# The scores across two chunks in two 32-column pieces: a hybrid recurrence and ConvFFN layer on one core

## The chip, the cores and the metric

The kernel runs on one core of a Trainium2 chip. The metric is the device time of one execution in microseconds (us). Given are the times of three executions of the kernel before and one profiled execution, from which all rows below come.

## The reference

One layer over 2048 tokens of width 1024, all in fp32. After a modulated RMSNorm one projection feeds two gated linear attentions, 4 HGRN heads with 128 key features and 4 GLA heads with 64, each with 128 value features. Both are computed in chunks of 64 tokens:

```python
b = jnp.cumsum(g, axis=3)
scores = jnp.einsum('bhncd,bhnsd->bhncs', q * jnp.exp(b - ref), k * jnp.exp(ref - b))
scores = jnp.where(causal, scores, 0.0)
o = jnp.einsum('bhncs,bhnse->bhnce', scores, v)
...
s0 = jnp.zeros((B, H, DK, DV), jnp.float32)
_, s_prev = lax.scan(step, s0, (decay, u))
o = o + jnp.einsum('bhncd,nbhde->bhnce', q * jnp.exp(b), s_prev)
```

The heads are normed, gated and projected, and a second norm, an up projection with a causal convolution of width 3, a gated product and a down projection follow.

## The kernel before

The 2048 tokens are four sub-sequences of T = 512, each of NT = 4 token tiles of P = 128 tokens, that is two chunks of CH = 64. Two sub-sequences go through the token mixer (`plan_A`), then both through the ConvFFN (`plan_ffn`), and this twice. The large projections (L363, L849, L884, L1220, L1551) are matmuls in float32r with 512 moving columns, in three passes over operands split into a high and a low part; the split of the weights is a cast on ScalarE (L128) and a subtraction on VectorE (L131).

In `plan_A` a list of steps holds the projections, and the stages of the heads are hung between them by step number (`at`, `at_half`). A `Unit` is one HGRN head, or two GLA heads that share 128 partitions (features 0 to 63 and 64 to 127). So a sub-sequence has 8 heads in 6 units. `stage_b` makes `kx` on POOL (L592), the keys of the first chunk of every tile with their decay to the chunk's end; `stage_c` makes `qx` on VectorE, the queries of the second chunk with their decay from its start. `stage_d` calls `scores` for the unit's first head and `stage_d2` for the second head of a GLA unit.

`scores` (L642) works over two chunks at once: for each token tile `p` it makes a 128 x 128 block of scores, keys on the PSUM partitions, queries on the columns, all four tiles of a head in one PSUM bank. The scores within a chunk (L649) are made in four pieces of HC = 32 key columns: each has a named place in the array, `tile_position=(lo, r0)`, writes the 32 partitions from `r0` on, and has 64 moving columns for `r0` = 0 and 64 and 32 moving columns for `r0` = 32 and 96 (the upper triangle alone is made). The scores across the two chunks, the first chunk's keys against the second chunk's queries (L657), are one piece of 64 key columns and 64 moving columns without a named place. All of these matmuls are in plain fp32. POOL then clears an SBUF tile (L665) and VectorE copies the valid scores into it under a mask (L670).

`stage_d2` makes the chunk pairs' state updates (L680) and VectorE forms the three states between the tiles (L690); `stage_e` makes the outputs from scores and values (L706) and from queries and states (L707).

The order on ScalarE and SyncE is that of the program. The order of TensorE, VectorE and POOL in the main loop is made by the framework when the program is built, from the program's order and its own estimates of durations. The framework also places the semaphores.

Of the kernel before, what the change touches and what calls it, by code (L numbers as in the profile page):

```python
# [17 lines left out]
P = 128  # L18
# [8 lines left out]
CH = 64  # L27
HC = CH // 2
# [34 lines left out]
def kernel(  # L63
# [26 lines left out]
    act, vec, pool, pe, sp = nc.scalar, nc.vector, nc.gpsimd, nc.tensor, nc.sync  # L90
# [14 lines left out]
    def slot(dt=F32):  # L105
        return slots.tile([P, T], dt, tag="s", name="s")
# [4 lines left out]
    def bank():  # L111
        return psp.tile([P, T], F32, tag="ps", name="ps")
# [433 lines left out]
    class Unit:  # L546
# [95 lines left out]
        def scores(self, hd):  # L642
            kt_t, qt_t = self.e2, self.e1
            lo, hi, v, col = hd["lo"], hd["hi"], hd["v"], hd["col"]
            sb = bank()
            for p in range(NT):
                for r0 in range(0, P, HC):
                    c0, c1 = p * P + r0, p * P + (r0 // CH + 1) * CH
                    pe.matmul(  # L649
                        sb[r0 : r0 + HC, c0:c1],  # L650
                        lhsT=kt_t[lo:hi, c0 : c0 + HC],
                        rhs=qt_t[lo:hi, c0:c1],
                        start=True,
                        stop=True,
                        tile_position=(lo, r0),
                    )
                pe.matmul(  # L657
                    sb[0:CH, p * P + CH : (p + 1) * P],
                    lhsT=self.kx[lo:hi, p, :],
                    rhs=self.qx[lo:hi, p, :],  # L660
                    start=True,
                    stop=True,
                )
            sct = slot().rearrange("p (n t) -> p n t", t=P)
            pool.memset(sct, 0.0)  # L665
            sv = sb.rearrange("p (n t) -> p n t", t=P)
            for c0 in range(0, P, HC):
                rs = slice(c0, c0 + HC)
                mk = mask[rs, c0:P].unsqueeze(1).broadcast_to([HC, NT, P - c0])
                vec.copy_predicated(sct[rs, :, c0:P], mk, sv[rs, :, c0:P])  # L670
            self.sct.append(sct)
# [1311 lines left out]
```

## Time and profile before

| | |
|---|---|
| three executions, us | 2404.80, 2405.66, 2408.79 (median 2405.66) |
| profiled execution, us | 2408.29 |
| its span, first to last instruction, us | 2406.6 |
| mean granted TensorE clock | 0.987 of full speed |
| busy TensorE matmul / VectorE / ScalarE / POOL, us | 2330.0 / 1841.0 / 1179.5 / 344.0 |

Engines: PE is TensorE's matmuls, PEld its weight loads, DVE VectorE, ACT ScalarE, POOL GpSimd, SP SyncE. L657 is line 657 of the kernel. An fp32 matmul shows as two loads and two matmul records. The matmuls are pipelined, so that records overlap and their ends are modelled; the starts are what the reader should compare. Waits are inferred from the semaphores' events.

### The profile page before, as it was taken

To read this page: it belongs to the slowest core of one execution; us is meant where nothing else is said; L and a number is where in the kernel's file an instruction comes from. 1 tells how busy PE (TensorE), PEld (TensorE's weight loads), DVE (VectorE), ACT (ScalarE), POOL (GpSimd) and SP (SyncE) were. 2 spreads that over 40 slices of the span, in tenths; PEclk is the share of its full clock that TensorE was granted. 3 is DMA by queue.
4 is the path that set the end of the run, shared out by engine and by line. 5 is a ranking of instruction groups with operands and counts; after the bars stand their busy time and mean duration, and the time that the engine had idled before them with its cause. 6 is when DMAs were issued, how large, how long until landed. Compare 5 with 4: busy or idle time off the path is not lost.

```text
span 2406.6 us, 32511 instructions
## 1 busy us (share of the span) xinstructions
PE 2330.0 (97%) x12054; PEld 1920.2 (80%) x12054; DVE 1841.0 (76%) x2787; ACT 1179.5 (49%) x2095; POOL 344.0 (14%) x312
## 2 busy tenths in 40 slices
PE   8999999999999999999989999999999999999996
PEld 6878787887888888888777878888878888888885
DVE  6786778868788788887876676566697787897778
ACT  5643544366454545544445354543654545545453
POOL 3342234110000000000124213320100000000001
PEclk9999999999999999999999999999999999999998
DMA  8332352323222247996434034221232222589761
GB/s 303 110 119 106 111 228 96 128 72 133 93 92 92 101 139 245 347 336 216 169 140 152 17 114 167 71 80 54 96 127 79 101 96 101 180 283 378 249 205 70
DMA packets 148703, 360.80 MB, mean 150 GB/s; under 512 B 17544, under 2 KB 20024, under 8 KB 148544
## 3 DMA queue, kind: packets, MB, share of 16 engines
q1 hardware_dynamic: 148544, 358.73, 41.9%
q8 instruction: 94, 1.54, 0.3%
q14 instruction: 65, 0.53, 0.1%
HBM read 293.65 MB, written 65.01 MB: 149 GB/s over the span
## 4 chain that ended last, share of the span: by engine, by line
PE 76%; DVE 14%; ACT 3%; issue 3%; DMA 3%; POOL 0%; SPq 0%; DVEq 0%; ACTq 0%; POOLq 0%
PE ps L1220 26%; PE ps L1551 14%; PE ps L363 13%; PE ps L849 12%; PE ps L884 3%; DVE wlo L131 2%; DVE s L131 2%; PE ps L657 1%; PE ps L649 1%; DMA s<-in_w_ada 1%; PE ps L706 1%; PE ps L707 1%; ACT whi L128 1%; DVE s L1666 1%; PE ps L680 1%
## 5 line engine op out<-in xcount | busy, mean ns | idle before, releaser
L1220 PE MATMUL ps<-s,whi 128*128 128x512 f32 x1904 | 585.9, 389 | 2.4 <-DVE big L1320 2.4
L363 PE MATMUL ps<-s,whi 128*128 128x512 f32 x1568 | 493.2, 396 | 11.8 <-ACT whi L128 11.8
L131 DVE TENSOR_TENSOR wlo<-big,whi 128x1024 fp32r<-128x1024 f32 (+3 forms) x290 | 343.1, 1193 | 137.7 <-ACT whi L128 134.2
L1220 PEld LDWEIGHTS ps<-s,whi 128*128 128x128 f32 x1904 | 357.2, 188 | 77.4 <-DVE big L1320 3.2
L1551 PE MATMUL ps<-s,whi 128*128 128x512 f32 (+1 forms) x1272 | 384.9, 384 | 4.7 <-DVE s L131 3.0
L1220 PE MATMUL ps<-s,wlo 128*128 128x512 f32 x952 | 370.0, 389 | 2.4 <-DVE wlo L1213 2.4
L363 PEld LDWEIGHTS ps<-s,whi 128*128 128x128 f32 x1568 | 295.4, 190 | 77.5 <-ACT whi L128 14.4
L128 ACT CAST whi<-big 128x1024 fp32r<-128x1024 f32 (+3 forms) x298 | 275.2, 939 | 148.0 <-PE ps L1551 27.9
L849 PE MATMUL ps<-whi,s 128*128 128x512 f32 (+2 forms) x1280 | 340.8, 355 | 6.2 <-ACT whi L128 6.2
L455 POOL TENSOR_TENSOR s<-s 128x512 f32<-128x512 f32 (+1 forms) x69 | 102.8, 1490 | 1552.6 <-ACT s L454 1134.2
L363 PE MATMUL ps<-s,wlo 128*128 128x512 f32 x784 | 308.1, 394 | 2.8 <-DVE wlo L131 2.8
L1551 PEld LDWEIGHTS ps<-s,whi 128*128 128x128 f32 x1272 | 237.3, 189 | 54.6 <-DVE s L131 4.7
L849 PEld LDWEIGHTS ps<-whi,s 128*128 128x128 f32 x1280 | 218.9, 190 | 38.5 <-ACT whi L128 7.9
L1551 PE MATMUL ps<-s,wlo 128*128 128x512 f32 (+1 forms) x636 | 244.1, 384 | 5.0 <-DVE wlo L131 4.9
L849 PE MATMUL ps<-wlo,s 128*128 128x512 f32 (+2 forms) x640 | 205.6, 352 | 7.0 <-DVE wlo L131 7.0
L1220 PEld LDWEIGHTS ps<-s,wlo 128*128 128x128 f32 x952 | 178.7, 188 | 40.6 <-DVE wlo L1213 3.2
L363 PEld LDWEIGHTS ps<-s,wlo 128*128 128x128 f32 x784 | 148.9, 190 | 35.7 <-DVE wlo L131 4.1
L1213 DVE TENSOR_TENSOR wlo<-big,whi 128x1024 fp32r<-128x1024 f32 (+1 forms) x136 | 145.4, 1085 | 5.9 <-ACT whi L1209 5.7
L1209 ACT CAST whi<-big 128x1024 fp32r<-128x1024 f32 (+1 forms) x136 | 127.5, 939 | 37.4 <-DVE big L1197 33.7
L1551 PEld LDWEIGHTS ps<-s,wlo 128*128 128x128 f32 x636 | 119.8, 188 | 30.2 <-DVE wlo L131 7.3
L1265 DVE SCALAR_TENSOR_TENSOR big<-big,cw_sb 128x1024 f32<-128x1024 f32 x68 | 87.4, 1285 | 68.4 <-ACT big L1257 68.4
L849 PEld LDWEIGHTS ps<-wlo,s 128*128 128x128 f32 x640 | 114.0, 190 | 22.5 <-DVE wlo L131 8.9
(220 smaller groups left out, 3294.4 us busy)
## 6 DMA issues: line engine op xcount, KB each, us to landing
big<-in_wt SPq DMA_DIRECT2D x230, 512.0 KB
s<-td SPq DMA_DIRECT2D x110, 256.0 KB
big<-in_wd SPq DMA_DIRECT2D x72, 384.0 KB
s<-actd SPq DMA_DIRECT2D x98, 256.0 KB
s<-in_w_ada SPq DMA_DIRECT2D x96, 256.0 KB
big<-in_wd SPq DMA_DIRECT2D x72, 320.0 KB
actd<-big SPq DMA_DIRECT2D x34, 512.0 KB
td<-s SPq DMA_DIRECT2D x54, 256.0 KB
```

Source lines behind the costliest of these rows:

```text
L128: act.copy(hi, src)
L131: (lo_engine or vec).tensor_tensor(lo, src, hi.bitcast(F32), op=ALU.subtract)
L363: pe.matmul(pt, lhsT=wv[:, k * P : (k + 1) * P], rhs=hv, start=(n == 0), stop=(n == 3 * KD - 1))
L455: engine.tensor_tensor(acc, acc, sq, op=ALU.add)
L649: pe.matmul(sb[r0 : r0 + HC, c0:c1], lhsT=kt_t[lo:hi, c0 : c0 + HC], rhs=qt_t[lo:hi, c0:c1], start=True, stop=True, tile_position=(lo, r0),)
L849: pe.matmul(pt[:, 0 : c1 - c0], lhsT=hv[:, tt * P : (tt + 1) * P], rhs=wv[:, k2 * stride + c0 : k2 * stride + c1], start=(m == 0), stop=(m ...
L884: pe.matmul(pout[j][0], lhsT=wv[:, k * P : (k + 1) * P], rhs=hv, start=(k == 0 and m == 0), stop=(k == KD - 1 and m == 2),)
L1209: act.copy(dst[f][0][:, 0:n], src[f][:, 0:n])
L1213: vec.tensor_tensor(lo[:, 0:n], src[f][:, 0:n], hi[:, 0:n].bitcast(F32), op=ALU.subtract)
L1220: pe.matmul(pt, lhsT=wv[:, c0 : c0 + P], rhs=hv, start=(start and n == 0), stop=(n == 11), skip_group_check=not start)
L1265: vec.scalar_tensor_tensor(t_, src[:, 1 : 1 + D], w1, t_, op0=ALU.mult, op1=ALU.add)
L1551: pe.matmul(pt[:, cols], lhsT=wv[:, ki * P : (ki + 1) * P], rhs=hv[:, cols], start=(start and n == 0), stop=(n == 3 * np_ - 1), skip_group ...
```

## The change

The piece across the chunks becomes two pieces of 32 key columns, each with a named place in the array, in the same way as the pieces within a chunk. The second loop runs over `r0` = 0 and 32; both pieces stream the same `qx`.

```diff
@@ -654,13 +654,15 @@
                         stop=True,
                         tile_position=(lo, r0),
                     )
-                pe.matmul(
-                    sb[0:CH, p * P + CH : (p + 1) * P],
-                    lhsT=self.kx[lo:hi, p, :],
-                    rhs=self.qx[lo:hi, p, :],
-                    start=True,
-                    stop=True,
-                )
+                for r0 in range(0, CH, HC):
+                    pe.matmul(
+                        sb[r0 : r0 + HC, p * P + CH : (p + 1) * P],
+                        lhsT=self.kx[lo:hi, p, r0 : r0 + HC],
+                        rhs=self.qx[lo:hi, p, :],
+                        start=True,
+                        stop=True,
+                        tile_position=(lo, r0),
+                    )
             sct = slot().rearrange("p (n t) -> p n t", t=P)
             pool.memset(sct, 0.0)
             sv = sb.rearrange("p (n t) -> p n t", t=P)
```

## Rows read from the trace of the kernel before

**Rows 1.** The page: the chain that ended last, by engine and by line.
```profile
PE 76%; DVE 14%; ACT 3%; issue 3%; DMA 3%; POOL 0%; SPq 0%; DVEq 0%; ACTq 0%; POOLq 0%
PE ps L1220 26%; PE ps L1551 14%; PE ps L363 13%; PE ps L849 12%; PE ps L884 3%; DVE wlo L131 2%; DVE s L131 2%; PE ps L657 1%; PE ps L649 1%; DMA s<-in_w_ada 1%; PE ps L706 1%; PE ps L707 1%; ACT whi L128 1%; DVE s L1666 1%; PE ps L680 1%
```

**Rows 2.** Windows of two mixer stages: length; busy PE, PEld, DVE, ACT, POOL; clock; DMA.
```profile
136.00:250.00 114.00, 112.07 (x865) 91.47 (x863) 82.44 (x179) 50.18 (x136) 28.58 (x33) 1.00 0.30 107
400.00:515.00 115.00, 114.04 (x887) 94.11 (x886) 87.30 (x201) 47.01 (x129) 17.41 (x21) 1.00 0.34 115
```

**Rows 3.** Two source lines: records, shortest/median/longest ns, first and last start, forms.
```profile
L649 PE MATMUL ps<-s x1024: 192/216/243, 141.2 to 1657.1; 128*32 128x64 f32 x65, 64*32 64x64 f32 x63, 64*32 64x32 f32 x22, 128*32 128x32 f32 x21
...
L657 PE MATMUL ps<-s x256: 218/244/270, 141.5 to 1657.4; 128*64 128x64 f32 x64, 64*64 64x64 f32 x64
```

**Rows 4.** TensorE's timeline, first HGRN block (start us, us, rows*columns, moving operand, count).
```profile
141.22 0.31 PE L649 MATMUL ps<-s 128*32 128x64 f32 x8
141.47 0.33 PE L657 MATMUL ps<-s 128*64 128x64 f32 x2
141.73 0.31 PE L649 MATMUL ps<-s 128*32 128x64 f32 x8
...
143.23 0.50 PE L849 MATMUL ps<-whi,s 128*128 128x512 f32 x1
```

**Rows 5.** The same in windows of 0.02 us: last passes of a group alone.
```profile
141.31 0.23 PE L649 MATMUL ps<-s 128*32 128x64 f32 x2
...
141.32 0.22 PE L649 MATMUL ps<-s 128*32 128x64 f32 x1
...
141.57 0.22 PE L657 MATMUL ps<-s 128*64 128x64 f32 x1
```

**Rows 6.** TensorE's timeline, first GLA block.
```profile
165.64 0.31 PE L649 MATMUL ps<-s 64*32 64x64 f32 x8
165.88 0.32 PE L657 MATMUL ps<-s 64*64 64x64 f32 x2
...
167.62 0.50 PE L363 MATMUL ps<-s,whi 128*128 128x512 f32 x1
```

**Rows 7.** TensorE's timeline: first of 16 output passes, and what follows them.
```profile
155.15 0.27 PE L706 MATMUL ps<-s 128*128 128x128 f32 x1
...
156.85 0.48 PE L849 MATMUL ps<-whi,s 128*128 128x512 f32 x1
```

**Rows 8.** TensorE's timeline: state updates of a GLA unit, 16 passes in two column positions.
```profile
172.54 1.09 PE L680 MATMUL ps<-s 128*64 128x128 f32 x16
...
173.36 0.28 PE L680 MATMUL ps<-s 128*64 128x128 f32 x2
173.57 0.50 PE L363 MATMUL ps<-s,whi 128*128 128x512 f32 x1
```

**Rows 9.** Windows around the GLA units, sub-sequences 1 to 3; columns as in rows 2.
```profile
164.90:178.30 13.40, 13.40 (x143) 10.39 (x142) 13.14 (x20) 4.41 (x7) 3.40 (x6) 1.00 0.56 210
...
420.00:442.20 22.20, 22.20 (x206) 17.92 (x204) 21.55 (x38) 10.05 (x25) 7.81 (x9) 1.00 0.35 120
...
1352.30:1365.30 13.00, 13.00 (x140) 10.02 (x139) 12.56 (x19) 4.33 (x6) 3.25 (x5) 1.00 0.01 2
```

**Rows 10.** Timelines: a GLA unit's last state (L690) and the load taking it (L707).
```profile
177.27 0.34 DVE L690 SCALAR_TENSOR_TENSOR sprev<-sprev,dp,ps 128x128 f32<-128x128 f32 x1
...
178.35 0.30 PEld L707 LDWEIGHTS ps<-sprev,s 128*128 128x128 f32 x2
...
438.92 0.34 DVE L690 SCALAR_TENSOR_TENSOR sprev<-sprev,dp,ps 128x128 f32<-128x128 f32 x1
...
439.35 0.30 PEld L707 LDWEIGHTS ps<-sprev,s 128*128 128x128 f32 x2
...
1363.00 0.73 DVE L690 SCALAR_TENSOR_TENSOR sprev<-sprev,dp,ps 128x128 f32<-128x128 f32 x2
...
1365.60 0.30 PEld L707 LDWEIGHTS ps<-sprev,s 128*128 128x128 f32 x2
```

## The prediction

> **What bounds the kernel now.** The page comes first. The chain that ended last is TensorE for 76% of the span, and the score matmuls stand in it by name: L657, the piece across the chunks, and L649, the pieces within a chunk, hold about 1% each [rows 1]. Then the busy time by stage: in the stretch of the token mixer that holds eight score blocks TensorE is busy 112.07 of 114 us, VectorE 82.44, and the second sub-sequence looks the same [rows 2]. So here TensorE's queue sets the pace, and VectorE has a quarter of the time free on average. Then the two lines: L649 has 1024 matmul records, L657 256 [rows 3]. The loops issue 512 and 128, so each fp32 matmul here runs as two passes. 32 units (4 sub-sequences, 8 heads) each run one block of four token tiles: 8 + 2 passes per tile, 40 per block.
>
> **Where a block's time goes.** In the timeline a block of an HGRN head takes 2.01 us, from 141.22 to 143.23, in four equal periods of 0.50 us: eight passes of L649, two of L657, eight of L649 again [rows 4]. In narrower windows the last of the eight L649 passes starts at 141.32, only 0.10 us after the first, and then nothing starts until L657 at 141.47. The second pass of L657 starts at 141.57, and the next tile's L649 only at 141.73 [rows 4, 5]. So a period is 0.10 us in which the diagonal passes start, 0.15 us to the change of form, 0.10 us between the passes of L657, and 0.16 us to the change back. The GLA heads do the same with 64 rows: 165.64 to 167.62, 1.98 us [rows 6]. After the first piece no semaphore can explain the gaps: they repeat to 0.01 us in every tile, and only the form of the piece changes there (32 or 64 columns of the array).
>
> **What a pass costs.** Sixteen fp32 passes with 128 moving columns start between 155.15 and 156.85: 0.106 us each, 0.83 ns a column [rows 7]. So 64 moving columns are 0.053 us and 32 are 0.027. The wide second pass of a tile starts some 0.08 us after the first (141.31 against 141.22, rounded) [rows 4, 5]: one load of 32 columns, 0.027, and one pass of 0.053. The last pass of a form started 0.15 us before the next form; less its own 0.053 this leaves 0.10 us of emptying. That is paid twice a tile.
>
> **The change, part by part.**
> Removed: 128 matmuls, so 256 loads of 64 columns and 256 passes. Added: 256 matmuls, so 512 loads of 32 columns and 512 passes of 64 moving columns. The passes are those of L649 in form and position. The operands (kx, qx), the bank, the wait of the first piece and the reader (L670) stay; no DMA and no step on another queue is added or moved.
> The eight changes of form in a block become one at its start and one at its end, which are there already. What then bounds a tile is the busiest column position. Position 0 gets two diagonal passes and two cross passes of 64 columns, 4 x 0.053 = 0.213 us; position 32 gets 2 x 0.027 + 2 x 0.053 = 0.160; positions 64 and 96 get 0.107 and 0.053. If positions run side by side, a block is 0.027 + 16 x 0.053 + 0.10 = 0.98 us.
> The nearest row for such a stream is L680 of the GLA units: 16 passes of 128 moving columns in two named column positions, all of one form. Its last starts at 173.36, and the block takes 172.54 to 173.57, 1.03 us [rows 8]. My rule gives 0.053 + 8 x 0.106 + 0.10 = 1.00, so it is 0.03 short, and one after the other they would need 1.7 us. I therefore take 1.00 us for the new block.
> Gain on TensorE's queue: 16 x (2.01 - 1.00) + 16 x (1.98 - 1.00) = 31.8 us.
> Bounds: no block can be shorter than position 0's passes, 0.85 us, which gives at most 36.6 us. If the cross pieces start only when the diagonal ones are done, but without emptying, a tile is 0.10 + 0.053 + 0.08 + 0.06 = 0.29 us, a block 1.26, the gain 23.5 us. I take the value at the L680 row because it has the same structure.
>
> A rule that speaks for the whole gap: the Trainium skill, "TensorEngine Tiling (Array Packing)", Key Properties, says that a change of the tiling mode drains TensorE while a change of tile within a mode doesn't. The rows show the gaps and not their cause; by that rule all of them go.
>
> **What is late next.** The 31.8 us are gained only where TensorE's later work isn't waiting for VectorE. There is one place per sub-sequence where VectorE is full: 13.14 of 13.40 us from 164.9, 21.55 of 22.20 from 420, 12.56 of 13.00 from 1352.3 [rows 9], with two GLA blocks (2 us of gain) inside. Behind them TensorE's load for L707 takes the state that VectorE's L690 writes. In the first sub-sequence that state is done at 177.27 + 0.34 = 177.61 and taken at 178.35: 0.74 us of room, so 1.2 of the 2 us are lost. In the second it is 439.26 against 439.35, room 0.09, so 1.9 are lost. In the third 1363.73 against 1365.60, room 1.87, so some 0.2 are lost, and 0.3 is taken for each of the third and the fourth [rows 10]. Sum of losses 3.7 us. Elsewhere VectorE's gaps are waits for TensorE, so it follows. The weight splits and the DMAs are issued behind the same steps and move along.
> Result: 31.8 - 3.7 = 28.1 us. The profiled execution took 2408.29 us (span 2406.6), so 2380.2 for it. The median of the runs is 2.6 us lower, and I state 2378 us against that median.
>
> **The rivals.**
> *The gap isn't the form's.* If the emptying belongs to going from the diagonal pieces to the cross pieces (same bank, the same 64 partitions), it stays: a tile is 0.10 + 0.15 + 0.09 + 0.15 = 0.49 us, and 128 tiles save 1 to 2 us: 2404, no measurable change. Against it: L680's passes go through one bank and the same partitions with no gap [rows 8]. Chance 5%.
> *Slower: the gap stays, and the two cross pieces also run one after the other,* because both stream the same moving operand qx. Place: TensorE's queue between a tile's last diagonal pass and the next tile. A tile is then 0.10 + 0.15 + 0.027 + 4 x 0.053 + 0.10 = 0.59 us against 0.50, and 128 tiles add 11.5 us: 2417. It decides only if both hold, since without the gap four serial passes (0.24 us) still cost less than today's 0.40 from 141.32 to 141.73. Against it: in L649 passes of four positions start within 0.10 us, where one after the other they would need 0.32 [rows 4, 5]. Chance 4%.
> *Loads block each other.* If a load waited for every running pass, each of 24 load-and-pass pairs in a tile would stand alone, 12 x 0.027 + 8 x 0.053 + 4 x 0.027 = 0.86 us, +46 us: 2452. Rows 4 and 5 show eight loads and passes begun in 0.10 us, so it doesn't hold for column positions. Chance 1%.
> The Trainium skill, "TensorE: Matmul & The Clock Gate", Part 3, states that rule: loads overlap running matmuls only where the row group differs, and all pieces of a block here share theirs. The L649 rows disagree.
> *Half of it:* no overlap between cross and diagonal, the lower bound above; 23.5 less 3.7 gives 2386. Chance 8%.
> That the change does nothing can be left out: the forms 128 x 64 and 64 x 64 at L657 are in the trace, and the added pieces ask for another.
>
> **How the numbers follow.** The forecast, a block near 1.0 us with losses of 2 to 8 us, has the other 82%: 2372 to 2384. The upper bound of the gain, 36.6 less 2, gives 2371; the half case with twice the losses gives 2390. The build also orders VectorE's, TensorE's and POOL's queues anew, and one displaced step costs what the waits around here cost, 1 to 2 us. So the range is 2370 to 2390. About 0.2% (4.8 us) is what a measurement of this kernel can tell from no change. Faster by more than that: forecast and half case, 0.90. Within: the first rival, 0.05. Slower: the two others, 0.05.
>
> **What would show it.** Right: L657 has 512 matmul records with 32 columns at about 0.22 to 0.24 us each; a block goes from 2.0 to about 1.0 us; the next line's first pass comes 0.15 us after the block's last; L707 gains short waits for L690 in the first and second sub-sequence; VectorE's busy sum doesn't change. Wrong: periods of some 0.5 us remain in the block, or the blocks shrink and TensorE waits for VectorE as much longer behind them.

## The result and the profile after

The changed kernel takes 2380.48 us (median of four executions, 2378.33 to 2382.34) against 2407.22 us before (four, 2404.80 to 2409.31): a ratio of 0.9895, with a 95% interval of 0.9883 to 0.9907, 26.7 us less. The forecast was 2378, in a range of 2370 to 2390, against the 2405.66 us that were known of the kernel before. The profiled execution took 2378.33 us, with a span of 2376.6 against 2406.6 before, 30.0 less.

The page of the changed kernel, which answers to rows 1: the score lines are no longer among the fifteen that lead the chain (lines behind 657 have moved by two: L851 is the L849 of before, L709 the L707, L692 the L690; L658 holds the cross pieces).

```profile
PE 74%; DVE 16%; ACT 4%; issue 4%; DMA 2%; POOL 0%; SPq 0%; DVEq 0%; ACTq 0%; POOLq 0%
PE ps L1222 26%; PE ps L1553 14%; PE ps L363 13%; PE ps L851 11%; PE ps L886 3%; DVE wlo L131 3%; DVE s L131 2%; DMA s<-in_w_ada 1%; PE ps L709 1%; PE ps L708 1%; ACT whi L128 1%; DVE s L1668 1%; PE ps L682 1%; PE ps L816 1%; DVE s L1579 1%
```

The source view of the cross pieces, which answers to rows 3: 512 passes in place of 256, all with 32 columns of the array.

```profile
L658 PE MATMUL ps<-s x512: 216/219/244, 139.6 to 1626.3; 128*32 128x64 f32 x86, 64*32 64x64 f32 x85
```

TensorE's timeline of the changed kernel, an HGRN block and the first GLA block, which answer to rows 4 and 6. The lines L649 and L658 now alternate every few hundredths of a microsecond:

```profile
209.60 0.30 PE L649 MATMUL ps<-s 128*32 128x64 f32 x7
209.70 0.22 PE L658 MATMUL ps<-s 128*32 128x64 f32 x1
...
210.35 0.22 PE L649 MATMUL ps<-s 128*32 128x64 f32 x1
210.38 0.30 PE L658 MATMUL ps<-s 128*32 128x64 f32 x3
210.62 0.50 PE L851 MATMUL ps<-whi,s 128*128 128x512 f32 x1
...
163.31 0.30 PE L649 MATMUL ps<-s 64*32 64x64 f32 x7
...
164.31 0.50 PE L363 MATMUL ps<-s,whi 128*128 128x512 f32 x1
```

The HGRN block takes 1.01 us from its first pass to the next line by the unrounded starts (210.62 - 209.60 = 1.02 by the rounded rows), where it took 2.00, and the GLA block 1.01 (1.00 by the rows), where it took 1.98. No gap is left inside.

**Where the 30 us come from.** TensorE issues the same other matmuls in both kernels, in the same order. So the start of each can be compared in the two traces, and the gain read as it grows. It grows in steps of 0.99 us behind each HGRN block and 0.97 behind each GLA block. The exception is the first block: there the build's new order put one projection pass (L851) between 40 of the 48 passes and the last 8, so it pays two more changes of form and gains 0.63:

```profile
140.17 0.33 PE L649 MATMUL ps<-s 128*32 128x32 f32 x3
140.42 0.50 PE L851 MATMUL ps<-whi,s 128*128 128x512 f32 x1
140.85 0.24 PE L649 MATMUL ps<-s 128*32 128x64 f32 x2
...
141.10 0.50 PE L851 MATMUL ps<-whi,s 128*128 128x512 f32 x1
```

The sum is 15 x 0.99 + 16 x 0.97 + 0.63 = 31.0 us. Between the blocks of a sub-sequence the gain falls again, by 1.10 us in the first, 1.95 in the second, 0.28 in the third and 0.28 in the fourth: 3.6 us. That leaves 27.4. (The 0.98 and 1.65 us named in an expectation below count only the passes that wait; behind each such stop the next pass comes 0.10 us later too, and that isn't made up.) The other 2.6 us of this pair of profiles lie outside these stretches, as the sum of rises and falls of up to 2 us. Most of them stand where the granted clock differs, as windows of both traces show (length, TensorE's busy time and matmuls, granted clock, DMA share and GB/s). Of the kernel before:

```profile
126.00:140.00 14.00, 11.06 (x39) 0.76 0.02 4
238.00:252.00 14.00, 12.07 (x56) 1.00 0.12 39
1425.00:1443.00 18.00, 16.07 (x69) 0.91 0.09 29
```

And of the changed kernel, at the same places of the program:

```profile
126.00:139.00 13.00, 10.63 (x43) 0.87 0.06 18
230.00:245.00 15.00, 13.05 (x55) 0.90 0.11 36
1404.00:1422.00 18.00, 16.05 (x77) 1.00 0.09 30
```

A mean of 0.76 is a mixture of the two levels, 2.4 and 1.2 GHz. TensorE is idle for 1.9 us or more in each of these windows in both kernels, but the lower level isn't at the same ones. Part of what the clock gives or takes comes back at a later wait: at some 1780 us of the kernel before, the changed one gained 1.1 us because it stood at the lower level for a shorter time there, and it lost 1.2 right behind, where its L1222 waited for a cast on ScalarE (L1211).

### The profile page after: what moved, and what is told of

Read it like the earlier page. It is cut to its first block, busy times and chain, and to the rows that moved or that the text cites. A ratio compares the mean times of both kernels' runs of the same rounds, so it can differ in the third digit from the quotient of the medians.

```text
span 2376.6 us, 33021 instructions
## 1 busy us (share of the span) xinstructions
PE 2299.3 (97%) x12310; PEld 1904.7 (80%) x12310; DVE 1838.8 (77%) x2787; ACT 1179.6 (50%) x2095; POOL 341.0 (14%) x312
## 4 chain that ended last, share of the span: by engine, by line
PE 74%; DVE 16%; ACT 4%; issue 4%; DMA 2%; POOL 0%; SPq 0%; DVEq 0%; ACTq 0%; POOLq 0%
PE ps L1222 26%; PE ps L1553 14%; PE ps L363 13%; PE ps L851 11%; PE ps L886 3%; DVE wlo L131 3%; DVE s L131 2%; DMA s<-in_w_ada 1%; PE ps L709 1%; PE ps L708 1%; ACT whi L128 1%; DVE s L1668 1%; PE ps L682 1%; PE ps L816 1%; DVE s L1579 1%
## 5 line engine op out<-in xcount | busy, mean ns | idle before, releaser
L1222 PE MATMUL ps<-s,whi 128*128 128x512 f32 x1904 | 586.2, 389 | 3.7 <-DVE big L1322 2.4
L363 PE MATMUL ps<-s,whi 128*128 128x512 f32 x1568 | 492.4, 396 | 11.8 <-ACT whi L128 11.8
L131 DVE TENSOR_TENSOR wlo<-big,whi 128x1024 fp32r<-128x1024 f32 (+3 forms) x290 | 343.6, 1194 | 134.4 <-ACT whi L128 130.6
L1222 PEld LDWEIGHTS ps<-s,whi 128*128 128x128 f32 x1904 | 357.0, 188 | 79.2 <-DVE big L1322 3.2
L1222 PE MATMUL ps<-s,wlo 128*128 128x512 f32 x952 | 369.9, 389 | 2.4 <-DVE wlo L1215 2.4
L363 PEld LDWEIGHTS ps<-s,whi 128*128 128x128 f32 x1568 | 294.9, 190 | 77.6 <-ACT whi L128 14.4
L851 PE MATMUL ps<-whi,s 128*128 128x512 f32 (+2 forms) x1280 | 339.9, 354 | 5.5 <-ACT whi L128 5.5
L363 PE MATMUL ps<-s,wlo 128*128 128x512 f32 x784 | 307.8, 394 | 3.1 <-DVE wlo L131 3.1
L851 PEld LDWEIGHTS ps<-whi,s 128*128 128x128 f32 x1280 | 218.2, 189 | 37.8 <-ACT whi L128 7.2
L851 PE MATMUL ps<-wlo,s 128*128 128x512 f32 (+2 forms) x640 | 205.0, 351 | 6.5 <-DVE wlo L131 6.5
L1222 PEld LDWEIGHTS ps<-s,wlo 128*128 128x128 f32 x952 | 178.7, 188 | 40.4 <-DVE wlo L1215 3.2
L363 PEld LDWEIGHTS ps<-s,wlo 128*128 128x128 f32 x784 | 148.6, 189 | 36.3 <-DVE wlo L131 4.9
L1211 ACT CAST whi<-big 128x1024 fp32r<-128x1024 f32 (+1 forms) x136 | 127.5, 939 | 37.4 <-DVE big L1199 33.8
L851 PEld LDWEIGHTS ps<-wlo,s 128*128 128x128 f32 x640 | 113.6, 189 | 21.9 <-DVE wlo L131 8.5
```

Source lines behind the costliest of these rows:

```text
L131: (lo_engine or vec).tensor_tensor(lo, src, hi.bitcast(F32), op=ALU.subtract)
L363: pe.matmul(pt, lhsT=wv[:, k * P : (k + 1) * P], rhs=hv, start=(n == 0), stop=(n == 3 * KD - 1))
L851: pe.matmul(pt[:, 0 : c1 - c0], lhsT=hv[:, tt * P : (tt + 1) * P], rhs=wv[:, k2 * stride + c0 : k2 * stride + c1], start=(m == 0), stop=(m ...
L1211: act.copy(dst[f][0][:, 0:n], src[f][:, 0:n])
L1222: pe.matmul(pt, lhsT=wv[:, c0 : c0 + P], rhs=hv, start=(start and n == 0), stop=(n == 11), skip_group_check=not start)
```

## The experiments

The kernel before was measured again beside them: 2405.51 us beside the first three variants and the paired heads, 2406.16 us beside the other three (medians of seven executions). The ratios below are to these.

**The name alone (one execution).** The piece across the chunks stays one of 64 columns and gets a named place.

```diff
                     rhs=self.qx[lo:hi, p, :],
                     start=True,
                     stop=True,
+                    tile_position=(lo, 0),
                 )
```

> The kernel before, with a named place (lo, 0) for the piece across the chunks, which stays one piece of 64 key columns. Theory F (TensorE empties itself at every change of form, 64 to 32 columns and back; pieces of one form run side by side): nothing changes, blocks of 2.01 and 1.98 us, time as before, 2407 us. Rival N (the name is what lets the piece run beside the others): blocks of about 1.0 us, 2380 us.

Measured: 2407.51 us. The timeline of this kernel has the periods of before, a block of 2.00 us:

```profile
140.14 0.31 PE L649 MATMUL ps<-s 128*32 128x64 f32 x8
140.39 0.33 PE L657 MATMUL ps<-s 128*64 128x64 f32 x2
140.64 0.31 PE L649 MATMUL ps<-s 128*32 128x64 f32 x8
...
142.15 0.50 PE L850 MATMUL ps<-whi,s 128*128 128x512 f32 x1
```

So the name does nothing by itself here, and N falls.

**The old pieces, grouped (four executions).** All four pieces of 64 columns stand behind the sixteen of 32.

```diff
                         tile_position=(lo, r0),
                     )
+            for p in range(NT):
                 pe.matmul(
                     sb[0:CH, p * P + CH : (p + 1) * P],
```

> The kernel before, with the four pieces across the chunks (64 key columns each, as before) behind all sixteen pieces within a chunk of the block. One change of form inside a block in place of seven. Theory F: diagonal part 0.027 + 8 x 0.053 + 0.10 = 0.55 us, cross part 0.053 + 8 x 0.053 + 0.10 = 0.58, a block of 1.13 us: 0.87 less than before, of which some 3 us in all are lost behind VectorE; 2407 - 32 x 0.86 + 3 = 2383 us. Rival W (a piece of 64 columns is slow in itself, 0.25 us for its two passes, wherever it stands): a block of 0.55 + 4 x 0.25 = 1.55 us, 2396 us.

Measured: 2383.78 us, ratio 0.9913 (95% interval 0.9896 to 0.9930). The timeline:

```profile
143.82 0.65 PE L649 MATMUL ps<-s 128*32 128x64 f32 x32
144.40 0.68 PE L658 MATMUL ps<-s 128*64 128x64 f32 x8
145.01 0.50 PE L850 MATMUL ps<-whi,s 128*128 128x512 f32 x1
```

32 passes of the one form, then 8 of the other, 1.19 us against 1.13 expected. Not one piece has changed, only the order, and most of the gain is there. The piece of 64 columns isn't slow: its eight passes take 0.61 us in a row, where two of them took 0.25 between changes of form. W falls.

**The other common form (four executions).** The scores within a chunk are made in pieces of 64 columns, and the cross piece is left as it was.

```diff
-                for r0 in range(0, P, HC):
+                for r0 in range(0, P, CH):
                     c0, c1 = p * P + r0, p * P + (r0 // CH + 1) * CH
                     pe.matmul(
-                        sb[r0 : r0 + HC, c0:c1],
-                        lhsT=kt_t[lo:hi, c0 : c0 + HC],
+                        sb[r0 : r0 + CH, c0:c1],
+                        lhsT=kt_t[lo:hi, c0 : c0 + CH],
```

> The kernel before, with the scores within a chunk in two pieces of 64 key columns and 64 moving columns, with named places, in place of four of 32; the piece across the chunks as before. All pieces of a block have the same form, and there are half as many as in the changed kernel. What is made in excess (keys after their queries) is masked as before. Theory F: position 0 has four passes of 64 moving columns per tile, as in the changed kernel; a block of 0.053 + 16 x 0.053 + 0.10 = 1.00 us; the time of the changed kernel, 2380 us. Rival W (only pieces of 32 columns run side by side): six passes of 0.107 us per tile, 2.6 us a block, 2425 us.

Measured: 2381.64 us, ratio 0.9904 (0.9886 to 0.9923), the time of the changed kernel within both intervals. Its timeline has L649 and L657 in one form and no gap (a block lasts 1.07 us):

```profile
139.66 0.34 PE L649 MATMUL ps<-s 128*64 128x64 f32 x4
139.82 0.22 PE L657 MATMUL ps<-s 128*64 128x64 f32 x1
139.83 0.27 PE L649 MATMUL ps<-s 128*64 128x64 f32 x1
139.88 0.22 PE L657 MATMUL ps<-s 128*64 128x64 f32 x1
```

So 32 columns aren't the point either. One form is.

**Two forms in two halves of the array (four executions).** The emptying could be local: a piece of 64 columns at position 0 takes columns that pieces of 32 at positions 0 and 32 still use. Here no piece of one form ever touches the columns of the other.

```diff
-                for r0 in range(0, P, HC):
+                for r0, w in ((0, CH), (CH, HC), (CH + HC, HC)):
                     c0, c1 = p * P + r0, p * P + (r0 // CH + 1) * CH
                     pe.matmul(
-                        sb[r0 : r0 + HC, c0:c1],
-                        lhsT=kt_t[lo:hi, c0 : c0 + HC],
+                        sb[r0 : r0 + w, c0:c1],
+                        lhsT=kt_t[lo:hi, c0 : c0 + w],
```

> The kernel before, with the two pieces at r0 = 0 and 32 within a chunk made as one piece of 64 key columns at position 0, while those at 64 and 96 stay pieces of 32. Pieces of 64 columns stand in the first half of the array alone, pieces of 32 in the second half alone. Theory F (any change of form empties the whole array): two changes per tile as before, of which one run is longer: 0.053 + 4 x 0.053 + 0.10 = 0.37 us and 0.027 + 2 x 0.053 + 0.10 = 0.23 us per tile, a block of 2.4 us, 2407 + 32 x 0.4 = 2420 us. Rival L (a piece waits only where it takes columns that pieces of another form still use): no gaps, position 0 has four passes of 64 moving columns per tile, a block of about 1.05 us, 2381 us.

Measured: 2423.96 us, ratio 1.0072 (1.0056 to 1.0089). The timeline shows a period of 0.60 us:

```profile
140.07 0.56 PE L649 MATMUL ps<-s 128*64 128x64 f32 x6
140.56 0.33 PE L657 MATMUL ps<-s 128*64 128x64 f32 x2
140.72 0.51 PE L649 MATMUL ps<-s 128*64 128x64 f32 x6
...
142.63 0.50 PE L849 MATMUL ps<-whi,s 128*128 128x512 f32 x1
```

A block takes 2.56 us. The six passes of an L649 row here are of both forms, two of 64 columns and then four of 32. Two narrow windows show the gap between them:

```profile
140.07 0.33 PE L649 MATMUL ps<-s 128*64 128x64 f32 x2
...
140.33 0.30 PE L649 MATMUL ps<-s 128*32 128x64 f32 x4
```

The second pass of 64 columns starts at 140.18 (140.07 + 0.33 less its own 0.22) and the first of 32 only 0.15 us later, though their columns are disjoint. So L falls: at a change of form no pass starts anywhere in the array for 0.15 us, wherever the pieces stand. The rule of the Trainium skill, "TensorEngine Tiling (Array Packing)", Key Properties, that a change of mode drains TensorE and a change of tile doesn't, agrees with this trace.

**VectorE's part in the losses (one execution of each).** Both kernels without most of the sums over `w_ada`, which stand on VectorE in the first two sub-sequences:

```diff
         for acc, raw in zip(ada_acc[j], ada_raw.pop((j, k))):
+            if k:
+                continue
             vec.scalar_tensor_tensor(acc, raw, c_sb[:, k : k + 1], acc, op0=ALU.mult, op1=ALU.add)
```

> The kernel before without the sums over w_ada behind the first row block (L229 runs for k = 0 only; 56 of its 64 calls on VectorE are left out, the loads stay). The modulation of the second norm and of the residuals is then another. It is the other half of a pair with the changed kernel without them. Both theories: somewhat under the kernel before, since VectorE is freed in the first two sub-sequences.

> The changed kernel without the sums over w_ada behind the first row block (as in its pair). Theory V (the losses behind the blocks, 0.98 us in the first sub-sequence and 1.65 in the second, come from VectorE being full there, and these sums fill it): against its pair the losses between the blocks fall to 0.2 to 0.3 us in each of the first two sub-sequences, as in the third and the fourth, where none of these sums stand. Rival S (the losses come from the order of the steps itself): 1.0 and 1.6 us as before.

Measured: 2403.66 and 2368.89 us. In the changed kernel TensorE's load for L709 waits for L692, as its timeline shows, which answers to the first two of rows 10:

```profile
174.00 0.34 DVE L692 SCALAR_TENSOR_TENSOR sprev<-sprev,dp,ps 128x128 f32<-128x128 f32 x1
174.39 0.30 PEld L709 LDWEIGHTS ps<-sprev,s 128*128 128x128 f32 x2 [0.71 <-DVE sprev L692]
174.86 0.33 DVE L692 SCALAR_TENSOR_TENSOR sprev<-sprev,dp,ps 128x128 f32<-128x128 f32 x1
175.24 0.30 PEld L709 LDWEIGHTS ps<-sprev,s 128*128 128x128 f32 x2 [0.33 <-DVE sprev L692]
```

In the view of TensorE's waits between 130 and 520 us (total, times, longest) that wait is new; the same view of the kernel before has no line for L707:

```profile
PE ps L709 <- DVE sprev L692: 1.4, 3, 0.7
PE ps L886 <- DVE s L131: 0.5, 1, 0.5
PE ps L363 <- DVE wlo L131: 0.3, 1, 0.3
```

Without the sums (the lines are L711 and L694 there) the timeline has the last two states formed in a row, and of the three loads only the first waits:

```profile
168.34 0.73 DVE L694 SCALAR_TENSOR_TENSOR sprev<-sprev,dp,ps 128x128 f32<-128x128 f32 x2
168.36 0.30 PEld L711 LDWEIGHTS ps<-sprev,s 128*128 128x128 f32 x2 [0.29 <-DVE sprev L694]
168.80 0.30 PEld L711 LDWEIGHTS ps<-sprev,s 128*128 128x128 f32 x2
169.24 0.30 PEld L711 LDWEIGHTS ps<-sprev,s 128*128 128x128 f32 x2
```

Compared step by step with its pair, the kernel loses 0.27 us between the blocks of the first sub-sequence and 0.28 in the second, where it lost 1.10 and 1.95; the third and the fourth, which hold none of these sums, lose 0.25 and 0.28. V holds. That is 2.5 us of the difference between the 34.8 us of this pair and 30. The rest isn't explained by it, since the granted clock and the waits at other places differ as well.

**The heads of a GLA unit in one block (four executions).** Their features are partitions 0 to 63 and 64 to 127, and their scores go to two banks. The pieces alternate:

```diff
-        def scores(self, hd):
+        def scores(self, hds):
...
-            sb = bank()
+            sbs = [bank() for _ in hds]
             for p in range(NT):
                 for r0 in range(0, P, HC):
                     c0, c1 = p * P + r0, p * P + (r0 // CH + 1) * CH
-                    pe.matmul(
+                    for hd, sb in zip(hds, sbs):
+                        lo, hi = hd["lo"], hd["hi"]
+                        pe.matmul(
...
-            for hd in self.heads[1:]:
-                self.scores(hd)
```

> The changed kernel, with the two heads of a GLA unit made in one block, piece by piece in turn; they have 64 rows each, 0 to 63 and 64 to 127, and a bank each. Theory F with rows as with columns (places with other rows run side by side too): 96 passes in about 1.05 us in place of two blocks of 1.01, so 0.97 us less for each of 8 units, 7.8 us on TensorE; part of it is lost behind VectorE where that is full, in the first two sub-sequences: 2374 to 2377 us. Rival R (places with other rows take turns): 2.0 us for both heads, the time of the changed kernel, 2380 us; slower by a few us if the second head's scores, which now come earlier, delay the matmuls behind them.

Measured: 2373.62 us (2373.28 to 2375.05), ratio 0.9865 (0.9850 to 0.9880): faster than both kernels, 6.9 us under the changed one's median, and the two intervals of the ratio just don't meet. The first pair's block in the timeline:

```profile
165.39 0.27 PE L650 MATMUL ps<-s 64*32 64x64 f32 x8
...
166.32 0.29 PE L661 MATMUL ps<-s 64*32 64x64 f32 x5
166.54 0.50 PE L363 MATMUL ps<-s,whi 128*128 128x512 f32 x1
```

And its waits between 130 and 520 us:

```profile
PE ps L711 <- DVE sprev L694: 2.8, 5, 0.7
...
PE ps L363 <- DVE wlo L131: 0.9, 1, 0.9
```

96 passes take 1.15 us (1.05 expected) in place of two blocks of 1.01, 0.87 us less for each of 8 units, 7.0 in all. Places in other rows run side by side as those in other columns do, so R falls. The waits show the price: TensorE now waits 2.8 us for the states, where it waited 1.4. Compared step by step with the changed kernel, 2.9 of the 7.0 us are lost again behind these blocks, in all four sub-sequences, and 4.1 stay. The profiled spans differ by 4.8 us (2371.8 and 2376.6). That the medians differ by 6.9 is not the 7.0 of the blocks: what lies between 4.1 and 6.9 isn't explained, and it is of the size of the scatter.

## Why the prediction was right

**What bounds the kernel.** TensorE's queue: the gain appears behind 31 of the 32 blocks at full size, 0.97 or 0.99 us, and behind the first with 0.63.

**The gap.** It was read as emptying at a change of form, and that is what the grouped pieces, the other common form and the two halves show, each within 0.06 to 0.16 us of what the rule gave for its block (1.13, 1.00 and 2.4 expected; 1.19, 1.07 and 2.56 measured; the 2.4 counted eight changes, but that block begins and ends with pieces of 64 columns and so has nine, the one at its end included). The prediction's count is off by one as well: a block had seven changes of form inside, and the eighth is the one at its end, which stays. Its sums don't use the count. The first rival, a gap between diagonal and cross pieces, falls with the changed kernel itself: its pieces follow each other in the same bank and partitions without one. The two slower rivals fall there as well, and so does the half case, a block of 1.26.

**The new block.** 1.00 us was taken from the L680 block [rows 8], 1.01 was measured. My own rule, 0.98, was a little short, as it was for L680; it was short in every experiment with a new block, by 0.06 to 0.16, so the nearest row was the better source.

**The sum on TensorE.** 31.8 expected, 31.0 found; the 0.36 lost in the first block by the new order was in no sum, only in the range. The rest is 0.01 to 0.02 us a block.

**The losses behind VectorE.** 1.2 + 1.9 + 0.3 + 0.3 = 3.7 expected at the GLA units, 1.10 + 1.95 + 0.28 + 0.28 = 3.6 found, and the sums over `w_ada` make the difference between the first two sub-sequences and the others. The mechanism was right too: a unit's last state is done at 177.61 before and at 175.19 in the changed kernel, 2.42 us earlier, when TensorE had gained 2.33 before the two blocks. VectorE gained next to nothing inside, and the room at its last state set what was lost. In the second sub-sequence it is the same: 439.26 and 431.78, 7.48 us against 7.53. But TensorE also stops earlier than the text had it, at the load of the second state (174.39); in the second sub-sequence 0.45 stands at L363, which waits for the weight split L131; and in the third and the fourth the stop is at the first state (done at 1349.00, its load at 1349.06), where the text looked only at the last.

**The total.** 28.1 us expected; 30.0 in the profiles, 26.7 between the medians. The blocks and losses make 27.4. The 2.6 us above it in the profiles stand for the most part where the granted clock differs, which the sum did not contain. For the medians the rest was not followed. That they come within 1.4 us of the 28.1 is in part luck: the four executions of the kernel before lie 4.5 us apart. VectorE's busy sum hardly changes (1841.0 to 1838.8 us), as said.

## What to carry to other kernels

When small matmuls are packed into parts of the array, the form (rows x columns of the array) that they share matters more than their size: here each change between 32 and 64 columns cost 0.10 us beyond the last pass, in which no pass started anywhere in the array, and a common form of 32 or of 64 columns served nearly equally (1.01 and 1.07 us a block). A change of the rows alone was not tested. Where forms can't be made equal, group the matmuls by form. Then look for pieces of the same form in other rows or columns that can be issued in turn, and check which engine the freed time makes late.

## What the runs showed of the hardware

Passes in different column positions with the same rows overlap, loads included, with starts some 0.01 us apart (eight in 0.10 us [rows 4, 5]). So do passes in different rows: 96 in 1.15 us.

The four executions of the changed kernel differ in the same order as their mean granted clock: 2378.33, 2379.18, 2381.79 and 2382.34 us at 0.988, 0.987, 0.986 and 0.985. So some 4 us of scatter may go with how long TensorE stood at 1.2 GHz, but it isn't shown: the four of the kernel with the paired heads don't keep that order (2373.50 us at 0.986, 2375.05 at 0.989). A gain of one or two microseconds can't be read from one execution here, while the steps behind the single blocks of a kind (the first apart) agree to 0.01 us.

Where a load had to wait for its operand, the next pass came later too: two neighbouring passes that started 0.12 us apart (178.01 and 178.13 in the kernel before) start 0.22 us apart behind such a wait (174.39 and 174.61 in the changed one).
